# An embedding gather with position add: each sequence stored in four transfers of every fourth partition instead of one, released one by one by successive adds

## The chip, the cores and the metric

The kernel runs on one core of a Trainium2 chip. The metric is the device time in microseconds (us), the median of a few runs. Before the change it was 184.11 us, the median of three runs from 184.02 to 184.17. Every run has a recorded span, a little shorter than its time: 182.4 us for the profiled run of the kernel before. The clock granted to TensorE was 1.0, and TensorE does almost nothing.

## The reference

```python
indices          # (32, 512) int32, values below 50000
embedding_table  # (50000, 512) float32
position_embed   # (512, 512) float32
token_embed = embedding_table[indices]
return (token_embed + position_embed).astype(np.float32)   # (32, 512, 512)
```

So 16,384 rows of 2 KB are fetched, a position row is added to each, and 33.5 MB are written. There are 33.5 MB to read and 33.5 MB to write.

## The kernel before

A sequence is 512 rows, held as 128 partitions times K = 4 rows, 1 MB. There are 24 slots of that size in SBUF. The pool engine (Pool) issues 128 gathers of 128 rows each; VectorE adds the position rows to each gathered part (128 adds); SyncE issues the stores. Each store waits for a count of adds on one semaphore.

```python
    stores = []
    for b in range(B):                       # B = 32 sequences
        if b <= 1 or b == B - 1:
            parts = QUARTERS                 # (1, 1, 1, 1): four stores of 256 KB
        elif b <= 5 or b == B - 2:
            parts = HALVES                   # (2, 2): two stores of 512 KB
        else:
            parts = (K,)                     # one store of 1 MB
        at = 0
        for n in parts:
            stores.append((b, at, n))
            at += n
    # ... cut: semaphores, loads of indices and positions, transposed indices ...
        for g in range(B * K):               # Pool: 128 gathers
            b, k = divmod(g, K)
            # ... cut: waits for the indices, and for the slot (24 sequences back) to be stored ...
            ins = nc.gpsimd.indirect_dma_start(out=slots[b % SLOTS][:, k, :], ...,
                ).then_inc(s_gather[g % LANES], 16)
            if g >= LANES:                   # at most 16 gathers in flight
                ins._wait_ge(s_gather[g % LANES], rounds(g - LANES))
        for g in range(B * K):               # VectorE: 128 adds of 128x512
            # ... cut ...
            nc.vector.tensor_tensor(out=part, in0=part, in1=pos_ps[k][:], op=add
                )._wait_ge(s_gather[g % LANES], rounds(g)).then_inc(s_add, 1)
        rest = 0
        for b, at, n in stores:              # SyncE: 46 stores
            done = s_out.get(b, s_rest)
            rest += done is s_rest
            nc.sync.dma_start(
                out=out_rows[b][:, at : at + n, :],
                in_=slots[b % SLOTS][:, at : at + n, :],
            )._wait_ge(s_add, b * K + at + n).then_inc(done, 16)
        nc.sync.wait_ge(s_rest, 16 * rest)
```

## Time and profile before

| | before |
|---|---|
| time, median | 184.11 us |
| recorded span | 182.38 us |
| last gather issued by Pool | 162.9 us |
| last add done | 172.3 us |
| last data packet ends | 174.51 us |
| from the last data to the end ("the closing") | 7.87 us |
| instructions in SyncE's part of the trace | 67 |

The page of the kernel before: its span, busy times, the DMA engines' busy tenths and GB/s in forty slices, the chain that ended last, the two costliest groups, and the stores.

```profile
span 182.4 us, 398 instructions
...
PE 0.7 (0%) x4; PEld 0.6 (0%) x4; DVE 87.1 (48%) x130; ACT 3.6 (2%) x5; POOL 121.8 (67%) x134
...
DMA  4999999999999999999999999999999999999910
GB/s 116 323 270 345 356 382 405 413 405 418 394 371 396 408 403 406 403 417 420 417 413 412 418 412 408 417 418 417 414 412 422 404 415 416 418 407 417 406 70 0
...
POOL 63%; issue 24%; DMA 6%; DVE 1%; SPq 0%; POOLq 0%
...
L121 POOL DMA_INDIRECT slot<-in_embedding_table_dram,idx_t x124 | 117.3, 946 | 37.8 <-issue 37.8
L150 DVE TENSOR_TENSOR slot<-slot,pos_ps 128x512 f32<-128x512 f32 x128 | 86.4, 687 | 80.0 <-issue 39.3
...
out_dram<-slot SPq DMA_DIRECT2D x24, 1024.0 KB
out_dram<-slot SPq DMA_DIRECT2D x10, 512.0 KB
out_dram<-slot SPq DMA_DIRECT2D x12, 256.0 KB
...
```

The DMA engines are busy nine tenths or more from the second slice to the 38th, and the rate is 404 to 422 GB/s in the second half, up to the 38th. Pool's gathers take 946 ns each, and at the issue rate of one per 1.25 us they cover the time up to 162.9 us. VectorE is 48% busy.

The end of the kernel before, in windows of 5 us. The columns are: length, busy time and number of instructions for PE, PEld, DVE, ACT and POOL, granted clock, DMA share, GB/s.

```profile
...
165.00:170.00 5.00, 0.00 (x0) 0.00 (x0) 2.07 (x4) 0.00 (x0) 0.00 (x0) 1.00 1.01 415
170.00:175.00 5.00, 0.00 (x0) 0.00 (x0) 1.37 (x2) 0.00 (x0) 0.00 (x0) 1.00 0.83 325
175.00:180.00 5.00, 0.00 (x0) 0.00 (x0) 0.00 (x0) 0.00 (x0) 0.00 (x0) 1.00 0.00 0
...
```

Data flow at the full rate (415 GB/s from 165 to 170 us) up to about 174.5 us and then stop; nearly 8 us pass before the span ends.

```profile
...
SPq L163 <- DVE slot L150: 8.0, 4, 5.6
...
```

An issue takes 0.33 us, and there are 46: SyncE looks idle.

### The profile page before, as it was taken

Reading aid. Unit: us, or ns where it says so; the run is one execution under the profiler, and the core shown is the slowest. Engines: PE = TensorE matmul, PEld = TensorE weight load, DVE = VectorE, ACT = ScalarE, POOL = GpSimd, SP = SyncE. Lnnn points to the kernel's source line nnn. Section 1 sums busy time; section 2 is a strip of 40 time slices with the busy share of each in tenths; the row PEclk is TensorE's granted clock in tenths of the full one; section 3 lists DMA queues with packets and bytes.
Section 4 is the critical chain, followed back from the end, with each engine's and each line's share of the span. In section 5 each row is a group of like instructions: output and inputs, shape, how many; then the busy total and the mean of one; then the engine's idle time right before and its main releaser. Section 6 shows DMA issues by size and latency. Waiting matters only on the chain.

```text
span 182.4 us, 398 instructions
## 1 busy us (share of the span) xinstructions
PE 0.7 (0%) x4; PEld 0.6 (0%) x4; DVE 87.1 (48%) x130; ACT 3.6 (2%) x5; POOL 121.8 (67%) x134
## 2 busy tenths in 40 slices
PE   0100000000000000000000000000000000000000
PEld 0100000000000000000000000000000000000000
DVE  0253635546545445738355644455474655454400
ACT  2500000000000000000000000000000000000000
POOL 3777777777777777777777777777777777750000
DMA  4999999999999999999999999999999999999910
GB/s 116 323 270 345 356 382 405 413 405 418 394 371 396 408 403 406 403 417 420 417 413 412 418 412 408 417 418 417 414 412 422 404 415 416 418 407 417 406 70 0
DMA packets 17634, 68.32 MB, mean 375 GB/s; under 512 B 3008, under 2 KB 3008, under 8 KB 14560
## 3 DMA queue, kind: packets, MB, share of 16 engines
q0 software_dynamic: 10240, 33.56, 48.4%
q1 hardware_dynamic: 7392, 34.74, 46.6%
q14 instruction: 2, 0.02, 0.0%
HBM read 34.74 MB, written 33.55 MB: 374 GB/s over the span
## 4 chain that ended last, share of the span: by engine, by line
POOL 63%; issue 24%; DMA 6%; DVE 1%; SPq 0%; POOLq 0%
POOL slot L121 63%; DMA slot<-in_embedding_table_dram,idx_t 5%; DVE slot L150 1%; DMA idx<-in_indices_dram 1%; POOLq L119 0%; SPq L193 0%; SPq L94 0%
## 5 line engine op out<-in xcount | busy, mean ns | idle before, releaser
L121 POOL DMA_INDIRECT slot<-in_embedding_table_dram,idx_t x124 | 117.3, 946 | 37.8 <-issue 37.8
L150 DVE TENSOR_TENSOR slot<-slot,pos_ps 128x512 f32<-128x512 f32 x128 | 86.4, 687 | 80.0 <-issue 39.3
L121 POOL DMA_INDIRECT slot<-in_embedding_table_dram,idx x4 | 4.0, 993 | 2.5 <-DMA idx<-in_indices_dram 1.6
L139 DVE CAST idx_f<-idx_raw 32x512 f32<-32x512 int32 x1 | 0.4, 415 | 4.5 <-DMA idx_raw<-in_indices_dram 4.5
L156 ACT COPY pos_ps<-pos_sb 128x512 f32<-128x512 f32 x4 | 2.3, 587 | 4.4 <-DMA pos_sb<-in_position_embed_dram 4.4
L156 ACT ACT_TABLE_LOAD x1 | 1.3, 1283 | 1.0 <-SPq L94 1.0
L133 PE MATMUL turned<-ident,idx_f 32*128 32x32 f32 x4 | 0.7, 307 | 4.9 <-DVE idx_f L139 4.9
L142 DVE CAST idx_t<-turned 128x128 int32<-128x128 f32 x1 | 0.3, 291 | 0.8 <-PE turned L133 0.8
L133 PEld LDWEIGHTS turned<-ident,idx_f 32*128 32x128 f32 x4 | 0.6, 208 | 4.9 <-DVE idx_f L139 4.9
L106 POOL MEMSET ones<- 32x32 f32 x1 | 0.1, 115 | 0.5 <-SPq L94 0.5
L182 POOL MEMSET const-float32-0.0<- 128x1 f32 x1 | 0.1, 103 | 0.3 <-issue 0.3
L107 POOL TENSOR_SCALAR_AFFINE_SELECT ident<-ones 32x32 f32<-32x32 f32 x1 | 0.2, 203 | 0.1
L182 POOL MEMSET const-uint8-127<- 128x1 uint8 x1 | 0.1, 120 | 0.0
L182 POOL MEMSET const-bfloat16-1.0<- 128x1 bf16 x1 | 0.1, 114 | 0.0
L182 POOL MEMSET const-float32-1.0<- 128x1 f32 x1 | 0.1, 106 | 0.0
## 6 DMA issues: line engine op xcount, KB each, us to landing
out_dram<-slot SPq DMA_DIRECT2D x24, 1024.0 KB
out_dram<-slot SPq DMA_DIRECT2D x10, 512.0 KB
out_dram<-slot SPq DMA_DIRECT2D x12, 256.0 KB
slot<-in_embedding_table_dram,idx_t POOLq DMA_INDIRECT x124
pos_sb<-in_position_embed_dram SPq DMA_DIRECT2D x4, 256.0 KB, 3.0
idx_raw<-in_indices_dram SPq DMA_DIRECT2D x1, 128.0 KB, 3.0
slot<-in_embedding_table_dram,idx POOLq DMA_INDIRECT x4
idx<-in_indices_dram SPq DMA_DIRECT2D x1, 4.0 KB, 1.7
```

The costliest lines, as they stand in the source:

```text
L106: nc.gpsimd.memset(ones[:], 1.0).then_inc(s_ident, 1)
L107: nc.gpsimd.affine_select(out=ident[:], in_=ones[:], pattern=[[-1, B]], compare_op=mybir.AluOpType.is_equal, fill=0.0, base=0, channel_mul ...
L121: ins = nc.gpsimd.indirect_dma_start(out=slots[b % SLOTS][:, k, :], out_offset=None, in_=table, in_offset=bass.IndirectOffsetOnAxis(ap=whe ...
L133: ins = nc.tensor.transpose(turned[:, k, :], idx_f[:, :, k], ident[:])
L139: nc.vector.tensor_copy(out=idx_f[:].rearrange("b p k -> b (p k)"), in_=idx_raw[:, :, 0])._wait_ge(s_raw, 16).then_inc(s_cast, 1)
L142: nc.vector.tensor_copy(out=idx_t[:], in_=turned[:])._wait_ge(s_turn, K).then_inc(s_idx, 1)
L150: nc.vector.tensor_tensor(out=part, in0=part, in1=pos_ps[k][:], op=add)._wait_ge(s_gather[g % LANES], rounds(g)).then_inc(s_add, 1)
L156: nc.scalar.copy(out=pos_ps[k][:], in_=pos_sb[k][:])._wait_ge(s_pos[k], 16).then_inc(s_ps, 1)
L182: nc = _bacc.Bacc("TRN2", target_bir_lowering=False, num_devices=1)
```

## The change

Intent: a 1 MB store comes at once, every 5 us, and then stores and gathers share the DMA engines unevenly: between 145 and 157 us of the trace before, stores are about 0.65 to 0.8 of the bytes for about 3.5 us of every 5, then hardly any for 1.5 us. Four transfers of 256 KB, each of 32 partitions and 8 KB per partition, released by four successive adds (the sequence's own last one and the first three of the next sequence), should spread the stores evenly between the gathers. The first and last sequences are stored in quarters by columns as before, sequences 1 and 2 in halves by columns and by partitions.

```diff
-HALVES = (2, 2)
-QUARTERS = (1, 1, 1, 1)
+COMBS = 4
...
-        if b <= 1 or b == B - 1:
-            parts = QUARTERS
-        elif b <= 5 or b == B - 2:
-            parts = HALVES
+        if b == 0 or b == B - 1:
+            split, combs = (1, 1, 1, 1), 1
+        elif b <= 2:
+            split, combs = (2, 2), 2
         else:
-            parts = (K,)
+            split, combs = (K,), COMBS
         at = 0
-        for n in parts:
-            stores.append((b, at, n))
+        for n in split:
+            for j in range(combs):
+                adds = min(b * K + at + n + j, B * K)
+                stores.append((adds, b, at, n, j, combs))
             at += n
+    stores.sort()
...
-        for b, at, n in stores:
+        for adds, b, at, n, j, combs in stores:
...
-                out=out_rows[b][:, at : at + n, :],
-                in_=slots[b % SLOTS][:, at : at + n, :],
-            )._wait_ge(s_add, b * K + at + n).then_inc(done, 16)
+                out=out_rows[b][j::combs, at : at + n, :],
+                in_=slots[b % SLOTS][j::combs, at : at + n, :],
+            )._wait_ge(s_add, adds).then_inc(done, 16)
```

All in all 128 stores of 256 KB take the place of 46 stores of 256 KB to 1 MB. (A wait of Pool also counts the stores of a slot by another field of the list; that changes nothing else.)

More of the change, by code (lines that the diff above doesn't have):

```diff
@@ L117 @@
             if b >= SLOTS and k == 0:
-                done = sum(1 for x in stores if x[0] == b - SLOTS)
+                done = sum(1 for x in stores if x[1] == b - SLOTS)
                 nc.gpsimd.wait_ge(s_out[b - SLOTS], 16 * done)
```

## The prediction

> **What bounds it now.** The DMA engines. In the page's forty slices they are busy 9 tenths or more from the second to the 38th; in windows of 10 us their share is 1.01 to 1.03 from 60 to 160 us, at about 415 GB/s. A second limit lies close: the pool engine issues the 128 gathers one every 1.25 us (0.95 busy, 0.30 issue), never held up, from 3.0 to 162.9 us. The gathers fall behind: the one issued at 159.45 landed 9.5 us later (chain that ended last). VectorE (48%) only follows. The end is tight: last add done at 172.3, data stop at about 174.1, then a fixed tail to 182.4.
>
> Single DMA packets in the trace have these median times: 4 KB gather packet 159 ns, 2 KB store packet 84, 4 KB 159, 8 KB 309, semaphore write 9. Over 16 engines the gathers are 81.4 us at the median (87.2 as they ran, with packets up to 1.65 us, all the longest in the first 80 us), the stores 82 to 84. That fills the span of 171 us.
>
> **How the queues share.** In steady state each 1 MB store comes at once, every 5 us. In 0.25 us stretches between 145 and 157 us, stores are 0.65 to 0.8 of the bytes for about 3.5 us, at 424 GB/s; then for 1.5 us only gathers run, falling from 412 to 387 GB/s. [...]
>
> **What the change does.** 128 stores instead of 46, 256 KB each, one released about every add (1.25 us).
> - Packets: 512 fewer of 2 KB (-2.7 us over 16 engines), 768 fewer of 4 KB (-7.6), 512 more of 8 KB (+9.9): -0.4 us.
> - 82 more stores, 1,312 more semaphore writes of 9 ns: +0.7 us.
> - Mixing: gather-only stretches become short (about 0.3 us, an estimate) and stay near 414. From 415 towards 420 GB/s over 130 us: -1.0 to -1.9 us. This is the only sizeable gain.
> - Stores come one to three adds later. With gathers queued this costs nothing, except from 9 to 15 us, where engines are not full (0.76 to 1.0): up to +0.5 us.
> - The tail holds more late stores, but engines stay busy through them: 0.
>
> SyncE's 128 issues of 0.33 us fit; slot waits stay slack. [...] I expect 8 KB packets to stay near 309 ns; no transfer of this shape is in the trace.
>
> **Prediction.** All lies on the DMA, hence on the critical path, but is small: 183.0 us, 8 in 10 between 181.2 and 184.6. Faster by over 2%: 0.07; within 2%: 0.89; slower: 0.04.
>
> **What would show it.** Stores' share of bytes near one half in every 0.5 us; gather packets at 159 to 161 ns rather than 164 in steady state; 8 KB packets still 309; steady GB/s 418 to 421; DMA ending near 173; gathers still issued until 162.9; adds evenly spaced rather than in groups.
>
> **What would make it wrong.** Slower: 32-partition transfers [...] (8 KB packets well over 320 ns), or a pause around each semaphore write. Faster: the long gather packets of the first 80 us are caused by store bursts and vanish (up to 4 us). More idle DMA from 10 to 30 us would cost at the end one for one.

-0.4, +0.7, -1.0 to -1.9, up to +0.5 and 0 come to between -1.6 and -0.2 us, and 183.0 lies 1.1 us below 184.11. That 8 KB packets of the new shape stay near 309 ns was my estimate from the 309 ns of the old one. Cuts of the same kind in the expectations below are marked.

## More of the kernel before

The shares of the chain add up to 94% of the span, so 6% (11 us) is put down to nothing.

SyncE's stores, by their line (shortest, median and longest in ns, then the first and last start), and then SyncE's own waits (total us, times, longest us):

```profile
...
L163 SPq DMA_DIRECT2D out_dram<-slot x46: 332/332/467, 9.2 to 172.3; - x46
...
```

```
174.918    33  COMPARE_BRANCH
175.076    17  EVENT_SEMAPHORE
175.168     7  DRAIN
175.841  1397  EVENT_SEMAPHORE
177.942   713  EVENT_SEMAPHORE
179.353   691  NOP
180.744   699  DRAIN
182.153     4  DRAIN
182.173     3  EVENT_SEMAPHORE
```

(Two more, of 11 and 17 ns, follow.) An instruction that does nothing (NOP) took 0.69 us, and from 177.942 us on each of the long ones is followed 1.4 us later by the next.

## The result, and the profile after

A ratio here is the mean time of one kernel's fast runs over that of the other kernel's fast runs in the same rounds, so it is not quite the ratio of the medians. "Fast" is the undisturbed state of a run; all runs were fast except one of a variant, which is named.

The changed kernel took 193.85 us (193.58 to 194.42, four runs), against 184.14 for the kernel before: 1.053 times, with a 95% interval from 1.0501 to 1.0559. The prediction was 183.0, with a range up to 184.6. It was wrong, and not only in size: the change is 5% slower.

The page after the change, the same parts:

```profile
span 192.7 us, 480 instructions
...
PE 0.7 (0%) x4; PEld 0.6 (0%) x4; DVE 87.8 (46%) x130; ACT 3.6 (2%) x5; POOL 122.1 (63%) x134
...
DMA  4989999999999999999999999999999999944460
GB/s 124 314 281 378 350 395 364 370 373 417 418 388 411 410 412 418 401 414 402 407 396 388 404 385 397 387 372 389 397 397 400 391 402 404 401 189 201 163 249 23
...
POOL 57%; issue 22%; DMA 4%; DVE 4%; POOLq 0%; SPq 0%
...
L125 POOL DMA_INDIRECT slot<-in_embedding_table_dram,idx_t x124 | 117.5, 948 | 37.8 <-issue 37.8
L154 DVE TENSOR_TENSOR slot<-slot,pos_ps 128x512 f32<-128x512 f32 x128 | 87.0, 688 | 76.4 <-issue 49.9
...
out_dram<-slot SPq DMA_DIRECT2D x128, 256.0 KB
...
```

Pool's gathers (948 ns) and VectorE's adds (688 ns) are as they were. In slices 36 to 39 the DMA engines are only 4 to 6 tenths busy, with 163 to 249 GB/s; before, they were full until they stopped. The shares of the chain now add up to 87%, so 13% of the span (25 us) is put down to nothing. The chain does not name SyncE, and still this is where the time went.

The end in windows of 5 us, columns as before:

```profile
...
165.00:170.00 5.00, 0.00 (x0) 0.00 (x0) 2.64 (x4) 0.00 (x0) 0.00 (x0) 1.00 0.86 353
170.00:175.00 5.00, 0.00 (x0) 0.00 (x0) 0.00 (x0) 0.00 (x0) 0.00 (x0) 1.00 0.44 184
175.00:180.00 5.00, 0.00 (x0) 0.00 (x0) 0.00 (x0) 0.00 (x0) 0.00 (x0) 1.00 0.45 184
180.00:185.00 5.00, 0.00 (x0) 0.00 (x0) 0.00 (x0) 0.00 (x0) 0.00 (x0) 1.00 0.50 198
185.00:190.00 5.00, 0.00 (x0) 0.00 (x0) 0.00 (x0) 0.00 (x0) 0.00 (x0) 1.00 0.44 169
...
```

From 170 us on VectorE and Pool have nothing left to do, and the DMA engines run at half or less (share 0.44 to 0.50): there is data to store and nobody issues it. Before that, the share hides the loss: from 100 to 150 us it is 1.01 at 391 GB/s after the change, and 1.02 at 414 GB/s before it. The SyncE lines:

```profile
...
L167 SPq DMA_DIRECT2D out_dram<-slot x128: 3/700/1478, 9.4 to 186.5; - x128
...
```

```profile
...
SPq L167 <- DVE slot L154: 9.6, 8, 3.6
...
```

```profile
...
140.06 46.74 SPq L167 DMA_DIRECT2D out_dram<-slot  x37
```

The first line says that the median issue takes 0.70 us instead of 0.33, and the last start is at 186.5 us, 17 us after the last add (169.0 us). The second says that only eight of 128 stores have a recorded wait for an add. The third groups 37 issues between 140.06 us and 186.8 us (140.06 + 46.74); such a group holds the pauses between its members as well, so what it shows is only that SyncE was still issuing long after the adds had ended.

From the trace I worked out how far each store's start lies behind the add that releases it, and how far apart the starts are:

```
store     starts at us   behind its add by us
  0 to 31    9 to 54            0.03
 32             55              0.28
 48             78              3.2
 64            101              6.8
 96            147             12.4
120            181             16.8
last start 186.48;  from store 32 on most starts are 1.40 to 1.44 us apart
(most durations: 0.70 us); adds come every 1.25 us
```

A store that takes 1.40 to 1.43 us against an add every 1.25 us falls behind a little each time. The start stamps themselves run late, too. The first packets of stores 114 to 121, near the end, move about 1.7 us before the start that the trace gives these stores. So the true backlog is about 15 us there. An engine share of 0.44 is 0.63 us of work in every 1.43 us.

The loss adds up in the profiled runs:

| | before | after | difference |
|---|---|---|---|
| last data packet ends | 174.51 us | 188.30 us | +13.8 |
| the closing | 7.87 us | 4.40 us | -3.5 |
| span | 182.38 us | 192.70 us | +10.3 |

The closing has become shorter: in the kernel after, SyncE's NOP took 0.02 us. The slow pace ended at 186.46 us, when the last three stores got their stamps within 0.03 us of each other.

So "SyncE is too slow for 128 stores" is read from the profile. Why it needs 1.4 us per store in one stretch of the trace and 0.33 in another is not, and that is what the experiments are about.

### The profile page after: what moved, and what is told of

Same layout as the page of the kernel before. It is cut to its first block, busy times and chain, and to the rows that moved or that the text cites. A ratio compares the mean times of both kernels' runs of the same rounds, so it can differ in the third digit from the quotient of the medians.

```text
span 192.7 us, 480 instructions
## 1 busy us (share of the span) xinstructions
PE 0.7 (0%) x4; PEld 0.6 (0%) x4; DVE 87.8 (46%) x130; ACT 3.6 (2%) x5; POOL 122.1 (63%) x134
## 4 chain that ended last, share of the span: by engine, by line
POOL 57%; issue 22%; DMA 4%; DVE 4%; POOLq 0%; SPq 0%
POOL slot L125 57%; DVE slot L154 4%; DMA slot<-in_embedding_table_dram,idx_t 3%; DMA idx<-in_indices_dram 1%; POOLq L123 0%; SPq L197 0%; SPq L98 0%
```

## The experiments

Theory A: SyncE can't keep up an instruction per 1.25 us for long, whatever the instruction. Rivals: B, the 32-partition shape makes the issue expensive; C, the shared completion semaphore with its many outstanding increments does; D, the transfers outstanding in SyncE's DMA queue hold up the next issue; E, the staggered release matters. In all there were 18 runs of 14 variants and the changed kernel itself; all gave correct results. (The texts for the fourth call use the letters D and E for two other theories, which they state.)

| kernel | chip | median us | before, same rounds | ratio (95%) |
|---|---|---|---|---|
| after | first | 193.85 | 184.14 | 1.053 (1.0501 to 1.0559) |
| two_queues | 7 | 188.62 | 184.15 | 1.0258 (1.0208 to 1.0309) |
| own_sem | 7 | 194.97 | 184.15 | 1.0582 (1.0536 to 1.0628) |
| blocks | 7 | 197.24 | 184.15 | 1.0635 (1.0552 to 1.0718) |
| columns | 7 | 187.21 | 184.15 | 1.017 (1.0151 to 1.0188) |
| combs2 | 8 | 187.03 | 184.4 | 1.0153 (1.0135 to 1.0171) |
| act_only | 8 | 190.69 | 184.4 | 1.0359 (1.033 to 1.0388) |
| tail_act | 8 | 184.35 | 184.4 | 0.9995 (0.998 to 1.0011) |
| waits | 8 | 190.21 | 184.4 | 1.0321 (1.0301 to 1.0342) |
| early_waits | 9 | 183.34 | 180.79 | 1.0152 (1.0128 to 1.0176) |
| combs1 | 9 | 181.06 | 180.79 | 1.0027 (0.9993 to 1.0061) |
| act_noise | 9 | 182.26 | 180.79 | 1.0086 (1.0064 to 1.0109) |
| pair_adds | 9 | 180.31 | 180.79 | 0.9979 (0.996 to 0.9997) |
| after_2 | 4 | 182.12 | 180.78 | 1.0082 (1.0052 to 1.0113) |
| waits_2 | 4 | 181.05 | 180.78 | 1.0031 (1.0 to 1.0061) |
| pair_adds_2 | 4 | 180.08 | 180.78 | 0.9966 (0.9941 to 0.999) |
| comb_mid | 13 | 191.11 | 184.15 | 1.0369 (1.0355 to 1.0383) |
| burst | 13 | 193.43 | 184.15 | 1.0496 (1.0482 to 1.0511) |
| columns_2 | 13 | 187.05 | 184.15 | 1.0156 (1.0141 to 1.0172) |

Read the fourth column first. The same kernel before takes 184.1 to 184.4 us on some chips and 180.8 on chips 4 and 9. I call the first kind slow-record chips and the second quick chips; the reason for the name follows. The two kinds answer differently to the same change, so a ratio is compared only with ratios of the same kind.

### First call, chip 7: which part of a store is dear

**two_queues.** Odd quarters are issued by ScalarE instead of SyncE.

```diff
-            nc.sync.dma_start(
+            (nc.scalar if j % 2 else nc.sync).dma_start(
```

> After, with every second comb transfer issued by ScalarE instead of SyncE; same transfers, same release. Theory A (SyncE needs about 1.4 us per 32-partition store when stores wait in line, so the issue of 112 of them is the new bound): each queue then needs 2 x 1.25 us of adds per issue, more than 1.4, so no store is issued late, the lag behind its add stays under 1 us, and the time falls from 193.9 to 181 to 184.5. Theory B (the transfers themselves are worse for the DMA engines[...]): nothing changes, 192 to 195. Theory C (the one semaphore shared by sequences 8 to 31 slows each issue): little changes, the time stays over 190.

Measured: 188.62 us, ratio 1.026, outside the expected range. The stores by issuing engine, and the end in windows of 5 us:

```profile
...
L167 SPq DMA_DIRECT2D out_dram<-slot x68: 332/468/934, 10.6 to 172.7; - x68
L167 ACTq DMA_DIRECT2D out_dram<-slot x60: 475/476/549, 17.6 to 171.2; - x60
...
```

```profile
...
170.00:175.00 5.00, 0.00 (x0) 0.00 (x0) 0.62 (x2) 0.00 (x0) 0.00 (x0) 1.00 0.86 338
175.00:180.00 5.00, 0.00 (x0) 0.00 (x0) 0.00 (x0) 0.00 (x0) 0.00 (x0) 1.00 0.01 2
...
```

Both engines now issue 0.03 us after the add up to 158 us (of the last 13 stores eight start later, by up to 2.07 us), and the data end at 175.12 us, close to the 174.51 us of the kernel before. So the late data were SyncE's pace and nothing in the DMA engines, the semaphores or the stagger. The steady rate was 416.7 GB/s against 414.5 before. But the kernel was not fast: its closing grew from 7.87 to 12.93 us. SyncE's closing instructions took 0.70 us a stamp, up to the very last (697 ns, at 187.36 us).

**own_sem.** Each sequence gets a completion semaphore of its own (rival C).

```diff
-    s_out = {b: sem(f"s_out{b}") for b in range(B - SLOTS)}
+    s_out = {b: sem(f"s_out{b}") for b in range(B)}
...
-        nc.sync.wait_ge(s_rest, 16 * rest)
+        for b in range(B - SLOTS, B):
+            nc.sync.wait_ge(s_out[b], 16 * sum(1 for x in stores if x[1] == b))
```

> After, with one completion semaphore for each sequence instead of one shared by sequences 8 to 31. The pace of the issues went from under 0.65 us to 1.40 us exactly where the shared semaphore comes in. Theory C (shared semaphore): issue pace falls back under 1.25 us all through, 181 to 184.5. Theory A (cost of the issue itself once they wait in line): still 1.4 us each, 193 to 195.

Measured: 194.97 us, ratio 1.058, most stores 1.40 to 1.46 us apart. Rival C falls.

**blocks.** The four transfers take 32 neighbouring partitions each instead of every fourth.

```diff
-                out=out_rows[b][j::combs, at : at + n, :],
-                in_=slots[b % SLOTS][j::combs, at : at + n, :],
+                out=out_rows[b][j * (P // combs) : (j + 1) * (P // combs), at : at + n, :],
+                in_=slots[b % SLOTS][j * (P // combs) : (j + 1) * (P // combs), at : at + n, :],
```

> After, with each transfer a block of 32 neighbouring partitions (64 in the two-way ones) instead of every fourth (second). Theory A1 (cost of issue by the partition stride): pace back under 0.65 us when in line, no lag, unless the DMA suffers [...] (then 8 KB packets grow well over 320 ns). Theory A2 (cost of issue by the count of stores or of their partitions, whatever the stride): 1.4 us each as before, 193 to 195.

Measured: 197.24 us, ratio 1.064 (one run of four, 198.41, was slow and is left out of the ratio). Packets of 8 KB took 356 ns on the mean, against 311.5 ns after the change, and up to 1421; the median stayed at 309. By the mean the stride of four in the change is therefore the better of the two, and the long packets that the prediction named as a danger (well over 320 ns) did not show in it. Why neighbouring partitions take longer is not shown. About SyncE's pace this run says nothing: its stores mostly start 0.5 to 2.2 us apart from 60 to 150 us, single issues last up to 2.75 us, and the DMA engines are full (share 1.01) at 386 GB/s, so something besides the pace of the issues holds this kernel back; what it is, is not shown.

**columns.** Every sequence in four column quarters of 128 partitions by 2 KB, as sequences 0 and 31 are anyway: also 128 stores, in another shape (rival B).

```diff
         elif b <= 2:
-            split, combs = (2, 2), 2
+            split, combs = (1, 1, 1, 1), 1
         else:
-            split, combs = (K,), COMBS
+            split, combs = (1, 1, 1, 1), 1
```

> Every sequence stored in four transfers of 128 partitions x 2 KB, each after its own add: the same 128 stores of 256 KB as after, another shape. Theory A by count (any store costs SyncE over 1.25 us once in line): lag grows as in after. Theory A by shape (the 32-partition form is dear, the 128-partition form costs the 0.33 us that before shows): lag stays near 0.03 us. The packets of 2 KB cost 84 ns against 309 for 8 KB, so by sums from the trace the DMA has about 7 us more to do: 187 to 192 if the issue is no limit.

Measured: 187.21 us, ratio 1.017; on chip 13 (below) 187.05. The time lies in the range expected for an issue that is no limit, but the starts show that it was one. From 58 us on the stores run at the same 1.40 us and fall 12.5 us behind their adds by 173 us. Rival B falls as an explanation of the pace: the shape is another, the number of instructions the same, the pace the same. Why this kernel lost only 3 us in the end is explained in part: its stores are released three adds (3.75 us) earlier, and at 1.40 us a store instead of 1.43 the last 88 gain about 2.6 us (an estimate from the two traces). The data end at 181.28 us instead of 188.30.

### Second call, chip 8: how many, and which engine

**combs2.** Two transfers per sequence instead of four.

```diff
-COMBS = 4
+COMBS = 2
```

> After with two transfers (every second partition, 64 x 8 KB) for each whole sequence instead of four: 72 stores instead of 128, one per 2.5 us. Theory A (SyncE cannot keep up more than one store per 1.40 us): no lag, stores issued within 0.1 us of their add, time back to 182.5 to 185. Theory B (cutting a sequence over partitions is itself bad for the DMA): clearly over 186.

Measured: 187.03 us, ratio 1.015. By the time alone theory B would be right ("clearly over 186"); the trace says otherwise. SyncE keeps up (stores start 0.03 us after their adds up to 161 us, the trace has 93 SyncE instructions instead of 149, and its data end at 174.96 us), but the closing is 10.84 us instead of 7.87. The price has moved behind the last data.

**act_only.** All stores from ScalarE.

```diff
-            nc.sync.dma_start(
+            nc.scalar.dma_start(
```

> After with all stores issued by ScalarE, which has nothing else to do after 9 us. If the limit of 1.40 us per store belongs to any queue that issues: same as after, 192 to 196, lag growing to 15 us or more. If it belongs to SyncE alone: no lag, and 180 to 184.

Measured: 190.69 us, ratio 1.036, in neither of the two expected ranges. ScalarE comes to the same pace, 0.70 us a stamp and mostly 1.40 to 1.47 us a store, but only from about 150 us on. So the pace isn't SyncE's own; why it sets in later on ScalarE is open. And SyncE, which issued nothing from 4 to 180 us here, still needs 0.70 us a stamp in its closing (NOP 710 ns), so its own earlier instructions are an unlikely cause of that.

**tail_act.** The kernel before, with the stores of the last two sequences from ScalarE. I then believed the closing to be work that the last stores leave with SyncE.

```diff
-            nc.sync.dma_start(
+            (nc.scalar if b >= B - 2 else nc.sync).dma_start(
```

> Before, with only the last six stores (sequences 30 and 31) issued by ScalarE. In before SyncE's own closing instructions (semaphore events, a NOP, drains) take 0.69 to 1.40 us each after its six last stores, but 0.01 to 0.03 us in after, where SyncE had been idle since the last store. Theory A' (each store leaves SyncE with 1.40 us of work that later instructions wait behind, whatever they are): those closing instructions become short, the stretch from the last landing to the end falls from 7.9 us to about 4.5 us, time 180 to 182. Otherwise (the closing is fixed): 184.

Measured: 184.35 us, ratio 0.9995, closing 7.88 us. SyncE issued nothing from 161 to 175 us, and still its closing instructions took 0.70 us a stamp. This belief of mine fell: the closing isn't what the last stores leave behind.

**waits.** The kernel before, with eight waits that are long fulfilled ahead of each store of sequences 8 to 23. No store is added, no data moves otherwise.

```diff
+            for _ in range(8 if 8 <= b < 24 else 0):
+                nc.sync.wait_ge(s_first, 16)
             nc.sync.dma_start(
```

> Before, with eight waits on SyncE that are long satisfied ahead of each of the stores of sequences 8 to 23 (one store per 5 us). If the pace of about 0.7 us holds for any SyncE instruction [...] (NOP and drains showed it in the closing of before): each store now costs 8 x 0.7 to 1.4 + 1.4 = 7 to 12.6 us against 5 us available, lag grows by 2 to 7 us per sequence, time 205 to 290. If only transfers cost 1.40 us: waits are nearly free, no lag, 184 to 186.

Measured: 190.21 us, ratio 1.032. The compiler merged the eight waits to four instructions, so my figures for eight were too high. The starts of SyncE's instructions around 75 us are 73.34 (a store), 74.74, 76.15, 77.54, 78.94 (four waits), 80.34 (the next store): each 1.40 us after the one before, 7.00 us a sequence, against 5 us that the adds take. The window from 85 to 160 us, here and in the run waits_2 on a quick chip (fourth call):

```profile
...
85.00:160.00 75.00, 0.00 (x0) 0.00 (x0) 40.85 (x61) 0.00 (x0) 56.71 (x61) 1.00 0.98 361
...
```

```profile
...
85.00:160.00 75.00, 0.00 (x0) 0.00 (x0) 40.26 (x60) 0.00 (x0) 56.72 (x61) 1.00 1.02 414
...
```

Here a wait that has nothing to wait for costs as much as a store, 1.40 us. SyncE has been made slow with no store added, so none of B, C, D and E is needed for the pace; theory A stands on this chip.

### Third call, chip 9, and the surprise

Four kernels were to sound the pace further: **early_waits** (80 such waits, merged to 40 instructions, right after the first load of the kernel before), **combs1** (the changed kernel with COMBS = 1), **act_noise** (the changed kernel with 128 tiny copies on ScalarE, each released by an add), and **pair_adds** (the kernel before with the adds of two gathers in one instruction, 68 adds instead of 128).

```diff
# early_waits, against the kernel before
         nc.sync.dma_start(out=idx0[:], in_=idx_first).then_inc(s_first, 16)
+        for _ in range(80):
+            nc.sync.wait_ge(s_first, 16)
# combs1, against the kernel after
-COMBS = 4
+COMBS = 1
# act_noise, against the kernel after
+        for g in range(8 * K, 24 * K):
+            for c in range(2):
+                at = 2 * g + c - 16 * K
+                nc.scalar.copy(out=scratch[:, at : at + 1], in_=ones[:, 0:1])._wait_ge(s_add, g + 1)
# pair_adds, against the kernel before (cut: a pair of gathers shares a semaphore)
-            part = slots[b % SLOTS][:, k, :]
+            n = 1 if alone(g) else 2
+            part = slots[b % SLOTS][:, k : k + n, :]
```

> Before, with eighty satisfied waits (about forty instructions, as pairs were merged in the earlier run with waits) on SyncE right after its first load, while the other engines are nearly idle. If SyncE can never do more than one instruction per 1.40 us [...]: those forty take about 50 us, and the time rises by 40 to 55 us, to 225 to 240. If the slow pace comes only once the rest of the core is busy: they take 0.03 to 0.1 us each, 2 to 4 us in all, and the time is 186 to 189.

> After with whole sequences in one transfer (COMBS = 1): only the start (sequence 1 and 2 in half-partition pieces, 3 to 5 whole) and sequence 30 (whole) differ from before. 44 stores, nothing waits on SyncE. My packet sums say within 0.5 us of before: 183.5 to 185.5. If the coarser start is itself a loss, the data end moves by over 1 us and the time is over 185.5.

> After, with 128 tiny copies on ScalarE, two per add of sequences 8 to 23 (55 to 135 us), which touch nothing of the rest. If SyncE's 1.40 to 1.43 us per store is its own limit: pace in that stretch unchanged, 193 to 195.5. If all engines share [...]: SyncE's pace there grows to 1.8 us or more, and the time goes over 200.

> Before with VectorE's adds made in pairs (128 x 1024) for sequences 1 to 30, 68 adds instead of 128, and sequence 1 stored in halves. DMA work as before; VectorE at 48% has room. [...] SyncE's closing gets quicker (7.9 us after the last data towards 4.4 us): 180.5 to 183. If not: data end later by up to 1 us because a pair waits for its second gather, 184 to 186.

(For act_noise and pair_adds read: if SyncE's pace depends on what ScalarE or VectorE does.)

Measured: on this chip the kernel before took 180.79 us. At most six of SyncE's instructions in a trace lasted 0.6 us or more (act_noise; in the first trace of the kernel after, with the same stores, 92 did). The 40 waits of early_waits took 2.4 us in all, after 1.2 us in which the first of them really waited for its load, and the time rose by 2.6 us (ratio 1.015); they say nothing of the slow chips. act_noise, which holds the whole change and 128 more instructions, was 1.009 times the kernel before instead of 1.053 or more. combs1 was within its interval (1.003), pair_adds a hair below (0.998). The expectations were made for a chip of the other kind and could not be tested here. That the loss depends on the chip had to be tested first.

### Fourth call, chip 4: the same kernels on a quick chip

**after_2** and **waits_2** are the changed kernel and waits, unaltered; **pair_adds_2** is pair_adds.

> After, unchanged, again. In the last job before itself took 180.8 us, not 184.1 to 184.4, and SyncE's closing instructions were short there: it ran on another chip (number 9; the earlier jobs on 7 and 8). Theory D (the 0.70 us per time stamp of SyncE is a matter of the chip or machine, and nearly all of the loss is it): on a chip where before takes about 180.8, after takes 181.5 to 183.5, no store is issued over 1 us late; on one where before takes 184.1 to 184.4, 193 to 195 with 1.43 us per store. Theory E (ScalarE's copies had somehow relieved SyncE in the last job): after takes 188 to 194 even where before takes 180.8.

> Before with eight satisfied waits ahead of each of 16 stores, again. Theory D: where before takes about 180.8 us, the waits cost 0.06 us each instruction and the time is within 0.5 us of before; where it takes 184, 190 as measured.

> Before with paired adds, again. Where before takes 180.8 us: 179.8 to 180.8, as in the last job. Where it takes 184: if fewer instructions on VectorE relieve SyncE's time stamps, 180 to 183; if not, 183.5 to 184.5.

Measured: after_2 182.12 us, ratio 1.0082; waits_2 181.05, ratio 1.0031; pair_adds_2 180.08, ratio 0.9966. The page of the changed kernel on this chip:

```profile
span 180.3 us, 480 instructions
...
DMA  3899999999999999999999999999999999999970
GB/s 117 314 265 364 324 390 375 367 377 374 401 415 402 414 410 416 417 419 410 419 417 419 407 417 422 410 418 417 414 414 415 413 421 418 415 417 409 428 274 1
...
POOL 66%; issue 22%; DMA 6%; DVE 0%; SPq 0%; POOLq 0%
...
out_dram<-slot SPq DMA_DIRECT2D x128, 256.0 KB, 5.5
...
```

The DMA engines are at nine tenths or more through the 38th slice. The chain's shares add up to 94% again, as in the kernel before. The end in windows of 5 us, and the stores' line:

```profile
...
165.00:170.00 5.00, 0.00 (x0) 0.00 (x0) 3.46 (x6) 0.00 (x0) 0.00 (x0) 1.00 1.02 418
170.00:175.00 5.00, 0.00 (x0) 0.00 (x0) 0.92 (x2) 0.00 (x0) 0.00 (x0) 1.00 0.88 347
175.00:180.00 5.00, 0.00 (x0) 0.00 (x0) 0.00 (x0) 0.00 (x0) 0.00 (x0) 1.00 0.02 9
...
```

```profile
...
L167 SPq DMA_DIRECT2D out_dram<-slot x128: 332/468/779, 9.3 to 171.9; - x128
...
```

An issue now takes 0.47 us at the median, the last start is at 171.9 us, and by my count each store starts 0.03 us after its add up to 168 us (of the last six, where two stores share an add, five start 0.1 to 1.05 us after it). The same two instruction streams of the runs waits and waits_2, on chip 8 and chip 4, in the timeline from 72 to 82 us (start, length, then the group):

```profile
...
73.34 7.70 SPq L165 DMA_DIRECT2D out_dram<-slot  x2
```

```profile
...
75.12 4.80 SPq L165 DMA_DIRECT2D out_dram<-slot  x2
```

In waits the group runs from the start of one store to the end of the next, with the four waits in between (the view does not list them), and takes 7.70 us, five times 1.40 and the 0.70 of the last. In waits_2 it takes 4.80 us, most of it SyncE waiting for the add: by the trace the four waits took 0.028 us each, 0.06 us apart. So the same instruction costs 1.40 us on chip 8 and 0.06 on chip 4.

The second difference between the two kinds of chips is in the record itself. SyncE's waits for the adds in after_2, waits, and waits_2:

```profile
...
SPq L167 <- DVE slot L154: 105.3, 116, 5.5
...
```

```profile
...
SPq L165 <- DVE slot L150: 21.2, 16, 2.7
...
```

```profile
...
SPq L165 <- DVE slot L150: 148.6, 46, 6.1
...
```

On chip 4 the record has 116 waits of the changed kernel's stores; the first trace had eight (shown above). All 46 stores of waits_2 have a wait, 16 in waits, four in the first trace of the kernel before. The waits took place; the record lost them. I counted the records of increments of the adds' semaphore, of which a complete trace holds 130:

```
slow-record chips   before 18, after 13, two_queues 15, own_sem 16, blocks 16, columns 13,
                    combs2 20, act_only 16, tail_act 21, waits 25, comb_mid 15, burst 14, columns_2 19
quick chips         early_waits, combs1, act_noise, after_2, waits_2: 130 each
                    (pair_adds and pair_adds_2, with 60 fewer adds: 70 each, complete)
landings of gathers, 2048 in a complete trace:
                    168 to 254 on the slow-record chips, 2048 in all seven traces of the quick chips
```

In 20 traces, with no exception, those with runs of stamps 0.70 us apart are those with lost records. (In the quick traces ten single issues last 0.6 to 1.03 us, with ordinary ones around them.) I suspect that on the slow-record chips the recording itself sets the pace. For it speak, in these traces, the pace per stamp (0.70 us) and not per kind of instruction (1.40 us for a store and for a wait), the end of the slow pace in one moment (three stamps within 0.03 us at 186.46 us), a NOP of 0.69 us, and start stamps that come about 1.7 us after the first packets. This is a guess and not shown: every timed run in these results has a recorded span, so there is no run of these kernels without recording, and I could not turn it off. What is shown is that the pace goes with the chip (or its condition on that occasion, which these runs can't tell apart); that on a slow-record chip more instructions of SyncE bring it on with no transfer added (waits); and that the same stores divided between two sequencers are free of it until about 170 us (two_queues). When it sets in and when it ends is not explained: in act_only SyncE's closing took 0.70 us a stamp (NOP 710 ns) though SyncE had issued next to nothing.

### Fifth call, meant for the rest on a quick chip, fell on chip 13

Three kernels were to split the 0.8% that the change costs on the quick chips. **comb_mid** keeps the splits of the kernel before for the first six and last two sequences and has the combs in between; **burst** takes the stagger away, so that four quarters are released together; **columns_2** repeats columns.

```diff
# comb_mid, against the kernel after
-        if b == 0 or b == B - 1:
+        if b <= 1 or b == B - 1:
             split, combs = (1, 1, 1, 1), 1
-        elif b <= 2:
-            split, combs = (2, 2), 2
+        elif b <= 5 or b == B - 2:
+            split, combs = (2, 2), 1
# burst, against the kernel after
-                adds = min(b * K + at + n + j, B * K)
+                adds = min(b * K + at + n, B * K)
```

> Before's stores for sequences 0 to 5, 30 and 31; after's four staggered combs for 6 to 29 alone. Where before takes 180.8 us: if the 0.8% that after loses there comes from the changed start and end (data 0.4 MB behind at 85 us, last data 1.4 us later), this equals before within 0.3% (180.3 to 181.3); if it comes from the combs of the steady state, 181.6 to 182.5. Where before takes 184: SyncE falls behind as in after, 191 to 194.

> After with all combs of a piece released at once by the sequence's own last add, nothing staggered: the same 128 transfers. Where before takes 180.8: the steady rate falls from after's 415.6 back to before's 414.5 GB/s if mixing is what the stagger buys (worth 0.3 us), but stores come one to three adds earlier, so the end is no later: 180.6 to 182. If the number or shape of the transfers costs, it stays at 182 to 182.5. Where before takes 184: 192 to 196.

> Four transfers of 128 partitions x 2 KB, each after its own add, again. Where before takes 180.8 us SyncE should not fall behind; the 2 KB packets make the stores cost 86 us of 16 engines against 82 to 84, so the end moves by at most 3 us, less what the early release gains (31.8 MB moved at 85 us against 31.4 before): 180.5 to 183. Where before takes 184: 187 as measured.

Measured: the chip was slow-record (before: 184.15 us; 14 to 19 of 130 records). comb_mid 191.11 us (1.037), burst 193.43 (1.050), columns_2 187.05 (1.016, as on chip 7). burst loses as much as the change does, so the stagger is not the cause of the loss (rival E). comb_mid has 139 SyncE instructions in its trace, and lies between the kernel before (67) and the change (149) in time; its data end at 185.31 us. The question of the 0.8% remained.

## Why the prediction was wrong, point by point

**The step that failed** is this one, in the prediction's words: "SyncE's 128 issues of 0.33 us fit; slot waits stay slack." I added up the recorded durations of 46 issues with long pauses between them (0.33 us) and concluded that 128 of them need 42 us of 171. (In after_2, on a quick chip, an issue of the new shape took 0.47 us at the median, 60 us in all, which would still have fitted.) On the chip of the verdict SyncE had 0.70 us per stamp once the first 32 stores were through: 1.40 to 1.43 us per instruction against an add every 1.25 us. The last data came 13.8 us later for it (1.4 us of which the change costs on a quick chip, too, see below), and the closing was 3.5 us shorter, +10.3 us of span in all. two_queues takes this away up to about 170 us and has the data back at 175.12 us; waits brings it about without a single added store; after_2 is the same kernel on a chip without it, and it costs 0.8%.

**"then a fixed tail to 182.4"** was wrong too. The tail of 7.87 us was not fixed: it was 4.40 us after the change, 10.84 in combs2, 12.93 in two_queues, and 4.26 on the quick chips (3.7 with paired adds). A closing of 7.87 us instead of 4.26 is also enough to account for the 3.4 us by which the kernel before differs between the two kinds of chips; no trace of it on a quick chip was kept, so this is read from the variants. The NOP of 0.69 us in the tail of the kernel before was the sign that I passed over.

**"The DMA engines" as the bound** was right for the kernel before (nine tenths or more from the second slice to the 38th, 414.5 GB/s), and for the changed kernel on a quick chip (415.6 GB/s from 85 to 160 us). Nor did it save the prediction: the engines were a bound only as long as SyncE fed them.

**Packets: right, the mixing in part.** In steady state gather packets took 161 ns on the mean in after_2 (predicted 159 to 161, from 164), and 8 KB packets 312 ns at the median (predicted 309). The stores' share of the bytes lay between 0.35 and 0.65 in 80% of the 1 us stretches from 60 to 160 us, but in only half of the 0.5 us stretches that the prediction named. The long gather packets of the first 80 us did not vanish: from 10 to 80 us the mean was 178.5 ns in after_2, 177.5 in the kernel before.

**"Mixing: ... -1.0 to -1.9 us. This is the only sizeable gain": too large.** Even mixing came, but from 85 to 160 us the rate was 415.6 GB/s in after_2 against 414.4 in waits_2, +0.3%, worth 0.2 us in 75 us. I had hoped for 420. Pool's gather every 1.25 us sets what can be moved in the long run: by my estimate 2 x 262,144 bytes per 1.25 us, 419 GB/s, 1% above the rate of the kernel before. More is possible only while a backlog lasts; at 85 us in after_2, by a count of packets, about 3.5 issued gathers were not yet moved and about 6.5 added parts of 256 KB not yet stored. The prediction named this second limit and did not set it against the gain.

**"Stores come one to three adds later ... up to +0.5 us": too small, by an observation that isn't settled.** At 40 us after_2 had moved 12.76 MB and waits_2 13.27 MB. The missing 0.51 MB are 1.2 us at 415 GB/s. All kernels with the start of the change had 12.76 to 13.09 MB there, all with the start of the kernel before 12.94 to 13.29, so the groups overlap (blocks, burst and early_waits, which alter the start in other ways, are left out).

**"The tail holds more late stores, but engines stay busy through them: 0": wrong by about 0.6 us on the quick chip.** By 160 us after_2 was 0.33 MB behind (0.8 us); its data ended at 176.04 us against 174.66, 1.4 us later.

On the quick chips the sum is thus about +1.2 at the start, -0.4 in between, +0.6 in the tail: +1.4 us. I worked this out from two traces and no experiment splits it, since the kernels meant for that fell on the other kind of chip. combs1, which has the start of the change but only whole stores, lost 0.27% with an interval that holds zero, so the start alone may cost less in time than the bytes suggest. This stays open. Even on these chips the direction was wrong: 0.6% faster was predicted and 0.8% slower measured. That 182.12 us lies inside the predicted range is luck, since the kernel before took 180.78 there.

**The dangers that the prediction named did not come.** No sign of longer packets (312 ns for 8 KB at the median) or of a pause after each semaphore write shows in after_2: the DMA engines' share from 85 to 160 us is 1.02 at 416 GB/s. The chance of 0.04 for "slower" rested on these two, and both were about the DMA engines.

No version beat both kernels by more than noise on every chip. pair_adds, 0.2 and 0.3% faster on the quick chips with intervals just below 1, was not run on a slow-record one.

## What to carry to other kernels

Count the instructions that a change gives to each sequencer, and compare the count with the time there is for each; here the 0.33 us of an issue, measured between long pauses, was not a rate that SyncE kept up on the chip of the verdict. Issues took 0.33 to 0.48 us at the median where the slow pace was absent (before, after_2, two_queues); where it held, the stores were mostly 1.40 to 1.47 us apart, from SyncE (after) and from ScalarE (act_only). Before trusting recorded durations, look at the instructions that do nothing (a NOP of 0.7 us) and at waits that must be there and are missing in the record (4 of 46): here both came in traces with stamps 0.70 us apart, and whether the recording takes part in what it measures is not shown. And run a change on a second chip before calling its price a property of the kernel: this one costs 5.3% on one kind and 0.8% on the other.
